# The norm folded into the router, the last two token tiles one by one, and VectorE's end ordered by hand, in a mixer and mixture-of-experts block

## The chip, the core and the metric

The kernel runs on one core of one Trainium2 chip. The metric is the device time of one launch in microseconds (us). The names in this text are those of the profile: PE is TensorE (PEld its weight load), DVE is VectorE, ACT is ScalarE, POOL is GpSimd, SP is SyncE. SP computes nothing here: it issues DMA transfers, one after the other, in the order of its program. POOL issues the indirect transfers and some plain ones.

## The reference

One post-norm layer over 1024 tokens of width 1024. A token mixer (differential attention beside a pooling mixer, merged by gates) ends in a product with `w_out`; then a layer norm, then a mixture of 32 experts in 4 groups of 8, then a second layer norm:

```
m   = merged @ w_out                                     # 1024x1024 @ 1024x1024
x1  = layer_norm(ALPHA * x + BETA * m)                   # ln1
g   = softmax(x1 @ w_router_group  + b_router_group)     # 4 groups, top 1
e   = softmax(x1 @ w_router_expert + b_router_expert)    # 8 experts of that group, top 2
f   = sum over the two chosen experts of
        weight * (silu(x1 @ w_gate[e]) * (x1 @ w_up[e])) @ w_down[e]      # width 512
out = layer_norm(ALPHA * x1 + BETA * f)                  # ln2
```

All values are float32. The kernel writes each wide product as three TensorE products of a high and a low part (`mm3`), and each weight is split into these parts on the chip by an ACT cast and a DVE subtraction (`split`).

## The kernel before

The mixer takes the first 800 us. What the change touches is the stretch behind it, here called the output stage, and what follows on it is the expert stage.

**Output stage.** The 1024 tokens lie in 8 tiles of 128. For a tile `j`, `mix` makes the product with `w_out` on PE in two halves of 512 columns (`n`), each over 8 blocks `k` with three matmuls into `pw`: 48 matmuls a tile. `residual` (DVE) adds `ALPHA * x` for one half and takes its statistics. After the second half `norm` calls `layer_norm` (DVE): mean and variance, a reciprocal root in steps, `x` minus mean times gain, a factor of -5/16 on the root, then two instructions of 512 columns for root and bias; POOL stores the tile to `X1`. Then come the routing steps of the tile:

- `turn`: 8 transposes on PE of the normalised tile (`px`), copied to `xT` by ACT; POOL scales the tile by `ALPHA` (L945) and stores it to `Y`, where the experts' results are added later.
- `route`: 8 matmuls (16 instructions in the trace) with the 36 router columns (`pr`, L820), then some 25 small DVE instructions that find the group, the two experts and the selection masks `M` and `Ms`; `weights` makes the two weights of the token.
- `places`: two small matmuls that count how many earlier tokens chose the same expert (L879, L880), and one-hot rows `ohr` (L884 to L890).
- `place`: matmuls that add the tile's tokens to the table `first` of each expert's tokens (L898), from which the indices `idx` for the experts' gathers are made at the end (L1013, L1014); for tiles 0 to 5 POOL stores the tile's rows of a table.

The order on PE and ACT is written out by hand: tiles are taken in the groups (0, 1), (2,), (3,), (4,), (5,), (6, 7), and the table `S5` says, for the last tile of a group, before which step `k` of its product a routing step stands. `S5_LATE` and `S5_END` hold what comes after the last product: both the transposes and the routing of tile 6, and all of tile 7's. DVE, POOL and SP are ordered by a scheduler.

**Expert stage.** Each expert takes 96 token rows: POOL gathers them from `X1` (L1089), PE transposes them (L1029), multiplies with gate and up (`gu`) and down (`dn`), and POOL adds the rows to `Y` by an indirect transfer (L1101). The weights of all experts come in 192 pieces of 1 MB (`we`, L1048), 6 an expert, all issued by SP in one queue. A piece waits in a buffer until ACT and DVE split it, in two halves, into one of 5 buffers `wh`. There are 16 buffers for pieces: 15 of a ring that the output stage also uses, and one more, `extra`, that takes piece 13 of every 16 (`M_AT`). Its memory lies where the output stage keeps small tensors and some of the split `w_out`:

```
w = slot([4, 512], F32, "we") if i % (NS + NM) not in M_AT else extra([4, 512], "we")
q = SP.dma_start(w, A["we"][expert[e], c].rearrange("p (k n) -> p k n", k=4))
```

The first 16 pieces are issued as early as their buffers come free, in the output stage. `layer_norm` of the second norm and the end follow after the last expert.

Of the kernel before, what the change touches and what calls it, by code (L numbers as in the profile page):

```python
# [57 lines left out]
S5_LATE = ((32, "turn", 6),)  # L58
S5 = {
    1: (),  # L60
    2: ((13, "turn", 0), (15, "route", 0)),
    3: ((1, "turn", 1), (3, "route", 1), (8, "places", 0), (11, "turn", 2), (13, "place", 0), (13, "route", 2), (14, "places", 1)),
    4: ((2, "place", 1), (4, "places", 2), (10, "turn", 3), (10, "place", 2), (12, "route", 3)),
    5: ((3, "places", 3), (10, "turn", 4), (10, "place", 3), (12, "route", 4)),
    7: ((3, "places", 4), (10, "turn", 5), (10, "place", 4), (12, "route", 5), (21, "places", 5), (26, "place", 5)) + S5_LATE,
}
S5_END = (("logits", 6), ("route", 6), ("turn", 7), ("weights", 6), ("logits", 7), ("route", 7), ("places", 6), ("weights", 7), ("place", 6), ("places", 7), ("place", 7))
# [12 lines left out]
P_GB, P_SUB, P_PS, P_N = 0, 16, 17, 21  # L80
# [26 lines left out]
def body(tc, ctx, A, out):  # L107
# [677 lines left out]
    def layer_norm(tiny, x, bs, y, g, b):  # L785

        mv = tiny([2], "mv")
        DVE.bn_aggr(mv, bs)
        v = tiny([4], "v")
        DVE.tensor_scalar(v[:, 0:1], mv[:, 1:2], EPS, None, op0=OP.add)  # L790
        steps = rsqrt_steps(v[:, 1:2], v[:, 0:1], v[:, 2:3])
        steps[0]()
        DVE.scalar_tensor_tensor(x, x, mv[:, 0:1], g, op0=OP.subtract, op1=OP.mult)
        steps[1]()
        steps[2]()
        DVE.tensor_scalar(v[:, 1:2], v[:, 1:2], -5.0 / 16, None, op0=OP.mult)
        for c in (slice(0, 512), slice(512, 1024)):
            DVE.scalar_tensor_tensor(y[:, c], x[:, c], v[:, 1:2], b[:, c], op0=OP.mult, op1=OP.add)

    wr = ph["S2"].tile([128, 8, 36], F32, name="wr")  # L800
    br = ph["S2"].tile([128, 36], F32, name="br")
    SP.dma_start(wr, A["wr"])
    SP.dma_start(br, bass.AP(tensor=A["br"].tensor, offset=0, ap=[[0, 128], [1, 36]]))

# [3 lines left out]
    def turned(x):  # L808
        xT1 = raw4([8, 128], "xT1")
        for g in range(2):  # L810
            px = p5.tile([128, 4, 128], F32, name=nm("px"), tag="X", bufs=2)
            for k in range(4):
                PE.transpose(px[:, k], x[:, (4 * g + k) * 128:(4 * g + k) * 128 + 128], ident)
            ACT.copy(xT1[:, 4 * g:4 * g + 4], px)
        return xT1

    def logits(xT1):
        pr = p5.tile([128, 512], F32, name=nm("pr"), tag="R", bufs=2)
        for k in range(8):
            PE.matmul(pr[:, :36], xT1[:, k], wr[:, k], start=k == 0, stop=k == 7)  # L820
        lg = tiny([36], "lg")
        DVE.tensor_add(lg, pr[:, :36], br)
        return lg, pr

    def route(j, lg, pr):

        s = tiny([16], "s")
        gm, ngm, sg = (s[:, i:i + 1] for i in range(3))
        DVE.tensor_reduce(gm, lg[:, 0:4], AX.X, OP.max)
        DVE.tensor_scalar(ngm, gm, -1.0, None, op0=OP.mult)  # L830
        eg, G = tiny([4], "eg"), tiny([4], "G")
        ACT.activation(eg, lg[:, 0:4], AF.Exp, bias=ngm, accum_out=sg)
# [3 lines left out]
        tg, fg = tiny([4], "tg"), tiny([1], "fg")  # L836
        DVE.tensor_reduce(mx[:, 0], le, AX.X, OP.max)
        DVE.scalar_tensor_tensor(tg, lg[:, 0:4], gm, down8[:, :4], op0=OP.is_equal, op1=OP.mult)
        for k in range(2):
            v = t[:, k]  # L840
            DVE.tensor_tensor(v, le, to(mx[:, k]), op=OP.is_equal)
            DVE.tensor_mul(v, v, down8[:, None, :].to_broadcast([128, 4, 8]))
            if k == 0:
                DVE.tensor_reduce(fg, tg, AX.X, OP.max)
                DVE.tensor_scalar(G, tg, fg, None, op0=OP.is_equal)
            DVE.tensor_reduce(f[:, k], v, AX.X, OP.max)
            DVE.tensor_tensor(oh[:, k], v, to(f[:, k]), op=OP.is_equal)
            if k == 0:
                big = tiny([4, 8], "big", bufs=1)
                DVE.scalar_tensor_tensor(big, oh[:, 0], NEG, le, op0=OP.mult, op1=OP.add)  # L850
                le = big
                DVE.tensor_reduce(mx[:, 1], le, AX.X, OP.max)
        M = tiny([2, NE], "M")
        for k in range(2):
            DVE.tensor_tensor(M[:, k].rearrange("p (g e) -> p g e", g=4), to(G), oh[:, k], op=OP.mult)
        Ms = tiny([NE], "Ms", BF)
        DVE.tensor_add(Ms, M[:, 0], M[:, 1])
        return M, Ms, pr, s, mx, G, eg

    def weights(j, s, mx, G, eg):  # L860

        gm, ngm, sg, me, gp, m1, m2, nm1, e2, w = (s[:, i:i + 1] for i in range(10))
        eq = tiny([2, 4], "eq", bufs=1)
        for k, m in enumerate((m1, m2)):
            DVE.scalar_tensor_tensor(eq[:, k], mx[:, k], 1.0, G, op0=OP.mult, op1=OP.mult, accum_out=m)
        DVE.tensor_reduce(me, eg, AX.X, OP.max)
        DVE.reciprocal(sg, sg)
        DVE.tensor_mul(gp, me, sg)
        DVE.tensor_scalar(nm1, m1, -1.0, None, op0=OP.mult)
        ACT.activation(e2, m2, AF.Exp, bias=nm1)  # L870
        DVE.tensor_scalar(w, e2, 1.0, None, op0=OP.add)
        DVE.reciprocal(w, w)
        DVE.tensor_mul(pay[:, j, 0, 2:3], w, gp)
        DVE.tensor_mul(pay[:, j, 1, 2:3], pay[:, j, 0, 2:3], e2)

    def places(j, M, Ms, pr):

        pp = pr[:, 256:288]
        PE.matmul(pp, tri, Ms, start=True, stop=False)  # L879
        PE.matmul(pp, one, cum, start=False, stop=True)  # L880
        oh = st([2, CAP + 2 * NE], "ohr")
        at = tiny([2], "at")
        for k in range(2):
            DVE.tensor_scalar(oh[:, k, CAP:CAP + NE], M[:, k], pay[:, j, 0, 3:4], None, op0=OP.mult)  # L884
            DVE.tensor_scalar(oh[:, k, CAP + NE:], M[:, k], pay[:, j, k, 2:3], None, op0=OP.mult)
        for k in range(2):
            t = tiny([NE], "pt", bufs=1)
            DVE.scalar_tensor_tensor(t, M[:, k], 1.0, pp, op0=OP.mult, op1=OP.mult, accum_out=at[:, k:k + 1])
        for k in range(2):
            DVE.tensor_scalar(oh[:, k, :CAP], slots, at[:, k:k + 1], None, op0=OP.is_equal)  # L890
        DVE.tensor_add(cum, cum, Ms)
        return M, pr, oh, at

    def place(j, M, pr, oh, at):
# [4 lines left out]
        DVE.tensor_add(first, first, pf.rearrange("p (c e) -> p c e", c=2))  # L899
# [5 lines left out]
        DVE.tensor_add(entry[:, j], sf, at)  # L905

# [26 lines left out]

    def norm(j):
        x = tl[j]["x"]
        layer_norm(tiny, x, tl[j]["s"], x, *lnp)
        POOL.dma_start(X1[j * 128:j * 128 + 128], x)

    def step(what, j):

        if what == "turn":
            x = tl[j]["x"]
            tl[j]["t"] = turned(x)
            y = slot2([D], F32, "yy") if j in Y_OUT else x
            POOL.tensor_scalar(y, x, ALPHA, None, op0=OP.mult)  # L945
            POOL.dma_start(Y[j * 128:j * 128 + 128], y)
        elif what == "route":
            if "l" not in tl[j]:
                tl[j]["l"] = logits(tl[j]["t"])
            tl[j]["m"] = route(j, *tl[j]["l"])  # L950
            if j < 6:
                weights(j, *tl[j]["m"][3:])
        elif what == "logits":
            tl[j]["l"] = logits(tl[j]["t"])
        elif what == "weights":
            weights(j, *tl[j]["m"][3:])
# [8 lines left out]
    with tc.manual_schedule(engines={mybir.EngineType.PE, mybir.EngineType.Activation}):  # L965
        for group in ((0, 1), (2,), (3,), (4,), (5,), (6, 7)):
# [4 lines left out]
            for n in range(2):  # L971
                for j in group:
# [355 lines left out]
def arrange(x, positions, w_in, gate_bias, lam_vecs, subln_gain, w_pool, pool_scale, w_branch_a, w_branch_b, w_out,  # L1328
# [56 lines left out]
    par[:, P_SUB] = a(subln_gain)[0]  # L1385
    par[:, P_PS:P_PS + 4] = a(pool_scale)[0].reshape(4, 128).T
# [29 lines left out]
```

## Time and profile before

| what | us |
|---|---|
| three runs: median (least, most) | 1566.15 (1562.53, 1566.98) |
| the profiled execution: its time, its span | 1564.77, 1563.0 |
| output stage, first to last start of a `pw` matmul | 808.8 to 923.49 |
| first gather of expert rows issued, first `gu` matmul | 942.58, 948.34 |
| last `dn` matmul of the expert stage | 1516.96 |
| PE busy in the span | 1488.5 (95%) |
| ACT waits for expert weights, 12 times in all | 8.4 |

Times of the trace count from the start of the span. The page's first lines give the busy time of each engine; a view by stretches gives the same for a window of time with the granted clock of TensorE and the share in which the core's 16 DMA engines were busy; the timeline gives single instructions, and in brackets how long the engine had been idle before one and what released it.

### The profile page before, as it was taken

The numbers are of one execution on the slowest core, as the hardware profiler recorded it, in microseconds if no ns is written. First come the engines' busy times: TensorE is split into PE (matmuls) and PEld (weight loads), VectorE is DVE, ScalarE is ACT, GpSimd is POOL, SyncE is SP. The second block draws the span as 40 slices with busy tenths as digits, with TensorE's granted clock in tenths as the row PEclk, the third lists the DMA queues.
The fourth block names the chain that finished last, engine by engine and source line by source line (L and its number), as shares of the span: only waits on it lengthen the run. The fifth ranks groups of instructions, "written<-read, shape, count | busy, mean of one in ns | idle before, by whom it ended". The sixth has DMA issues, their size and how long they took to land.

```text
span 1563.0 us, 22004 instructions
## 1 busy us (share of the span) xinstructions
PE 1488.5 (95%) x7627; PEld 1189.5 (76%) x7627; DVE 1195.1 (76%) x2284; ACT 945.3 (60%) x1571; POOL 277.3 (18%) x231
## 2 busy tenths in 40 slices
PE   8999999999999999999999988999999999999980
PEld 6988887798798898888888775777777777776750
DVE  5774214987988987775566788999989999898967
ACT  4323124665666766674341116888888888888864
POOL 0001000220210211100002544223222222211410
PEclk9999999999999999999999988999999999999995
DMA  6156224746856765618465477999999999999945
GB/s 237 56 175 201 81 75 101 222 152 170 231 184 176 215 188 144 150 67 312 150 256 208 171 261 256 383 370 375 375 374 356 362 364 357 366 352 377 396 147 215
DMA packets 116977, 375.46 MB, mean 240 GB/s; under 512 B 13767, under 2 KB 44871, under 8 KB 91504
## 3 DMA queue, kind: packets, MB, share of 16 engines
q1 hardware_dynamic: 76128, 303.25, 52.7%
q0 software_dynamic: 40160, 69.96, 17.3%
q8 instruction: 61, 1.00, 0.3%
q10 hardware_dynamic: 576, 0.83, 0.2%
q14 instruction: 52, 0.43, 0.1%
HBM read 312.44 MB, written 69.78 MB: 245 GB/s over the span
## 4 chain that ended last, share of the span: by engine, by line
PE 55%; issue 28%; POOL 9%; DVE 5%; ACT 1%; DMA 1%; POOLq 0%; DVEq 0%; SPq 0%; ACTq 0%
POOL Y L1101 7%; PE ps L570 4%; PE pg L162 4%; PE pg L163 4%; PE pg L164 4%; PE po L621 3%; PE pv L162 2%; PE pv L164 2%; PE pv L163 2%; PE tp L606 2%; POOL xg L1089 2%; PE pa L164 2%; PE pa L163 2%; PE pa L162 2%; PE pw L162 2%
## 5 line engine op out<-in xcount | busy, mean ns | idle before, releaser
L148 DVE TENSOR_TENSOR wh<-we,wh 128x1024 fp32r<-128x1024 f32 x384 | 459.7, 1219 | 54.1 <-ACT wh L147 50.5
L147 ACT CAST wh<-we 128x1024 fp32r<-128x1024 f32 x384 | 400.4, 1047 | 90.0 <-PE gu L164 51.5
L162 PE MATMUL gu<-wh,xT 128*96 128x512 f32 x512 | 204.3, 399 | 0.0
L164 PE MATMUL gu<-wh,xT 128*96 128x512 f32 x512 | 202.6, 396 | 0.6 <-DVE xT L148 0.6
L163 PE MATMUL gu<-wh,xT 128*96 128x512 f32 x512 | 201.8, 394 | 0.0
L1101 POOL DMA_INDIRECT Y<-y,idx x32 | 108.5, 3390 | 265.4 <-ACT y L1109 260.6
L148 DVE TENSOR_TENSOR w<-wraw,w 128x512 fp32r<-128x512 f32 x111 | 75.7, 685 | 92.1 <-ACT w L147 91.7
L147 ACT CAST w<-wraw 128x512 fp32r<-128x512 f32 x111 | 68.5, 621 | 115.1 <-PE pg L164 36.4
L573 ACT ACTIVATE P<-ps,stat 128x256 f32<-128x256 f32 (+7 forms) x128 | 94.8, 741 | 58.9 <-DVE stat L572 58.4
L164 PEld LDWEIGHTS gu<-wh,xT 128*96 128x96 f32 x512 | 83.0, 162 | 37.2 <-DVE xT L148 1.3
L163 PEld LDWEIGHTS gu<-wh,xT 128*96 128x96 f32 x512 | 83.3, 163 | 34.1 <-issue 0.5
L162 PEld LDWEIGHTS gu<-wh,xT 128*96 128x96 f32 x512 | 83.0, 162 | 33.2 <-ACT xT L147 0.2
L162 PE MATMUL dn<-wh,hT 128*96 128x512 f32 x256 | 102.4, 400 | 0.6 <-ACT hT L147 0.6
L570 PE MATMUL ps<-K,Q 128*128 128x512 f32 (+2 forms) x384 | 99.5, 364 | 1.2 <-DVE z L461 0.8
L164 PE MATMUL dn<-wh,hT 128*96 128x512 f32 x256 | 100.6, 393 | 0.0
L163 PE MATMUL dn<-wh,hT 128*96 128x512 f32 x256 | 100.6, 393 | 0.0
L162 PE MATMUL pg<-xT,w 128*128 128x512 f32 x256 | 100.4, 392 | 0.0
L163 PE MATMUL pg<-xT,w 128*128 128x512 f32 x256 | 100.0, 391 | 0.0
L164 PE MATMUL pg<-xT,w 128*128 128x512 f32 x256 | 99.9, 390 | 0.0
L572 DVE TENSOR_REDUCE stat<-ps 128x1 f32<-128x256 f32 (+7 forms) x128 | 95.3, 746 | 1.1
L570 PEld LDWEIGHTS ps<-K,Q 128*128 128x128 f32 x384 | 64.6, 189 | 10.8 <-DVE z L461 1.3
L162 PE MATMUL pv<-w,xT 128*128 128x256 f32 x256 | 72.8, 284 | 0.0
(277 smaller groups left out, 3395.3 us busy)
## 6 DMA issues: line engine op xcount, KB each, us to landing
we<-in_we_dram SPq DMA_DIRECT2D x192, 1024.0 KB, 23.5
wraw<-in_w_dram SPq DMA_DIRECT2D x61, 512.0 KB, 3.8
Q<-RQ POOLq DMA_DIRECT2D x64, 256.0 KB, 5.2
RQ<-rh SPq DMA_DIRECT2D x32, 256.0 KB, 3.3
K<-RK POOLq DMA_DIRECT2D x16, 512.0 KB, 5.5
V<-RV POOLq DMA_DIRECT2D x16, 512.0 KB, 5.7
OT<-ohl SPq DMA_DIRECT2D x48, 128.0 KB, 2.5
oT<-OT POOLq DMA_DIRECT2D x6, 1024.0 KB, 12.1
```

What stands on the lines that cost most here:

```text
L147: ACT.copy(hi, src)
L148: DVE.tensor_sub(lo, src, r(hi))
L162: PE.matmul(ps, a[0], b[0], start=start, stop=False)
L163: PE.matmul(ps, a[0], b[1], start=False, stop=False)
L164: PE.matmul(ps, a[1], b[0], start=False, stop=stop)
L570: PE.matmul(ps[:, c:c + n], q[:, o, m, qc], Kt[h, m][:, c:c + n], start=o == 0, stop=o == 1)
L572: DVE.tensor_reduce(st_[:, m:m + 1], ps[:, :W], AX.X, OP.max, negate=True)
L573: ACT.activation(Pt[h, i][m][:, :W], ps[:, :W], AF.Exp, bias=st_[:, m:m + 1], accum_out=st_[:, 2 + m:3 + m])
L606: PE.transpose(ps[:, k], p[:, (4 * g + k) * 128:(4 * g + k) * 128 + 128], ident)
L621: PE.matmul(o[:, 0, c], Vt[h][:, a, kt], aT[kt // 4][:, kt % 4, b, c], start=j == 0, stop=j == len(parts) - 1)
L1089: q = POOL.indirect_dma_start(out=x, out_offset=None, in_=X1, in_offset=IO(ap=idx[:, int(e < NXG), expert[e]:expert[e] + 1], axis=0), boun ...
L1101: q = POOL.indirect_dma_start(out=Y, out_offset=IO(ap=idx[:, 0, expert[e]:expert[e] + 1], axis=0), in_=y, in_offset=None, bounds_check=T - ...
```

## The change

It has three parts.

1. **The norm folded into the router.** `turn` transposes the tile before the norm (after the second residual). The router's weights are multiplied once by the gain (and by 5/16), on POOL, and `router`, 8 matmuls of 72 columns on PE, makes the column sums `wc` for the mean and the bias part that is added to `br`. `logits` becomes two DVE instructions (mean, then root and bias) in place of one. The factor of -5/16 is applied once to the gain, by ACT, and no more per tile. `centre` and `norm` follow the transposes.
2. **Tiles 6 and 7 one by one**, with a table `S5` that is new for all tiles. Tile 6's routing and half of tile 7's transposes stand between the products of tile 7.
3. **DVE's order written by hand** from tile 7's second residual on; `route` and `weights` are interleaved instruction by instruction, `entry` is made before `first`, and tile 7's scaling by `ALPHA` runs on ACT and no more on POOL.

```
-S5_LATE = ((32, "turn", 6),)
 S5 = {
     1: (),
-    2: ((13, "turn", 0), (15, "route", 0)),
...
-    7: ((3, "places", 4), (10, "turn", 5), (10, "place", 4), (12, "route", 5), (21, "places", 5), (26, "place", 5)) + S5_LATE,
+    2: ((3, "router", 0), (10, "turn", 0), (14, "route", 0)),
...
+    6: ((3, "places", 4), (4, "turn", 5), (8, "route", 5), (11, "place", 4)),
+    7: ((2, "places", 5), (4, "turn", 6), (7, "route", 6), (9, "place", 5), (11, "half", 7), (14, "places", 6)),
 }
-S5_END = (("logits", 6), ("route", 6), ("turn", 7), ("weights", 6), ("logits", 7), ("route", 7), ("places", 6), ("weights", 7), ("place", 6), ("places", 7), ("place", 7))
+S5_END = (("turn", 7), ("place", 6), ("centre", 7), ("root", 7), ("logits", 7), ("norm", 7), ("route", 7), ("places", 7), ("place", 7))
...
+    ACT.activation(lnp[0], lnp[0], AF.Copy, scale=-5.0 / 16)
...
+    wgb = slot([704], F32, "wgb")
+    w72, ones = wgb[:, :576].rearrange("p (k n) -> p k n", k=8), wgb[:, 576:]
+    POOL.memset(ones, 1.0)
+    for k in range(8):
+        g, b = (par[:, P_LN + 8 * i + k:P_LN + 8 * i + k + 1] for i in range(2))
+        POOL.tensor_scalar(w72[:, k, :36], wr[:, k], g, 5.0 / 16, op0=OP.mult, op1=OP.mult)
+        POOL.tensor_scalar(w72[:, k, 36:], wr[:, k], b, None, op0=OP.mult)
+    POOL.tensor_copy(wr, w72[:, :, :36])
+
+    def router():
+
+        pr = p5.tile([128, 512], F32, name=nm("pr"), tag="R", bufs=2)
+        for k in range(8):
+            PE.matmul(pr[:, :72], ones, w72[:, k], start=k == 0, stop=k == 7)
+        DVE.tensor_copy(wc, pr[:, :36])
+        DVE.tensor_add(br, br, pr[:, 36:72])
...
+    def turn(j, g):
+
+        x = tl[j]["x"]
...
+        px = p5.tile([128, 4, 128], F32, name=nm("px"), tag="X", bufs=2)
+        for k in range(4):
+            PE.transpose(px[:, k], x[:, (4 * g + k) * 128:(4 * g + k) * 128 + 128], ident)
+        ACT.copy(tl[j]["t"][:, 4 * g:4 * g + 4], px)
...
         lg = tiny([36], "lg")
-        DVE.tensor_add(lg, pr[:, :36], br)
+        mean, root = tl[j]["r"]
+        DVE.scalar_tensor_tensor(lg, wc, mean, pr[:, :36], op0=OP.mult, op1=OP.subtract)
+        DVE.scalar_tensor_tensor(lg, lg, root, br, op0=OP.mult, op1=OP.add)
         return lg, pr
...
+    def centre(j):
+        x = tl[j]["x"]
+        DVE.scalar_tensor_tensor(x, x, tl[j]["r"][0], lnp[0], op0=OP.subtract, op1=OP.mult)
+
     def norm(j):
-        x = tl[j]["x"]
-        layer_norm(tiny, x, tl[j]["s"], x, *lnp)
+        x, root = tl[j]["x"], tl[j]["r"][1]
+        for c in (slice(0, 512), slice(512, 1024)):
+            DVE.scalar_tensor_tensor(x[:, c], x[:, c], root, lnp[1][:, c], op0=OP.mult, op1=OP.add)
         POOL.dma_start(X1[j * 128:j * 128 + 128], x)
+        y = slot2([D], F32, "yy") if j in Y_OUT else x
+        if j == 7:
+            ACT.activation(y, x, AF.Copy, scale=ALPHA)
+        else:
+            POOL.tensor_scalar(y, x, ALPHA, None, op0=OP.mult)
+        POOL.dma_start(Y[j * 128:j * 128 + 128], y)
...
-        for group in ((0, 1), (2,), (3,), (4,), (5,), (6, 7)):
+        for group in ((0, 1), (2,), (3,), (4,), (5,), (6,), (7,)):
...
+                    if j == 7 and n:
+                        by_hand.close()
+                        by_hand.enter_context(tc.manual_schedule(engines={mybir.EngineType.PE, mybir.EngineType.Activation, mybir.EngineType.DVE}))
                     residual(j, n)
                     if n:
-                        norm(j)
+                        stats(j)
+                        if j < 7:
+                            root(j)
```

**What moves on SP.** The diff has no line on the loads of the expert weights, but SP's order is the scheduler's. These are SP's rows from the last load of `w_out` on, in the kernel before: pieces 0, 1, 2 and so on (`we_9574`, `we_9576`, ...), piece 12 (`we_9598`), piece 13 (`we_9631`, the one in the extra buffer) and piece 14.

```order
L198 DMA wraw_8114<-in_w_dram 128x1024 [waits DMAHW6_49,DMAHW5_49,DVE_49]
L1048 DMA we_9574<-in_we_dram 128x2048 [waits DMASW5_49,PE_49]
L1048 DMA we_9576<-in_we_dram 128x2048 [waits DMAHW7_49,PE_49]
L1048 DMA we_9578<-in_we_dram 128x2048 [waits DMAHW0_49,PE_49]
...
L1048 DMA we_9598<-in_we_dram 128x2048 [waits DMAHW2_49,DMASW2_49,PE_49]
L1048 DMA we_9631<-in_we_dram 128x2048 [waits DMAHW3_49,PE_49]
L1048 DMA we_9633<-in_we_dram 128x2048 [waits DMAHW4_49,DMASW3_49,PE_49]
```

In the changed kernel the same place reads as follows; `we_9666` is piece 13 (the extra buffer), `we_9609` is piece 0, `we_9633` piece 12 and `we_9668` piece 14.

```order
L199 DMA wraw_8114<-in_w_dram 128x1024 [waits DMAHW6_49,DMAHW5_49,DVE_49]
L1108 DMA we_9666<-in_we_dram 128x2048 [waits DVE_49,PE_49]
L1108 DMA we_9609<-in_we_dram 128x2048 [waits DMAHW7_49]
L1108 DMA we_9611<-in_we_dram 128x2048 [waits DMAHW0_49]
L1108 DMA we_9613<-in_we_dram 128x2048 [waits DMAHW1_49]
...
L1108 DMA we_9633<-in_we_dram 128x2048 [waits DMAHW3_49,DMASW2_49]
L1108 DMA we_9668<-in_we_dram 128x2048 [waits DMAHW4_49,DMASW3_49,PE_49]
```

Piece 13 has moved from behind piece 12 to the head of the queue, ahead of piece 0, and the waits for PE that pieces 0 to 12 had are no more on them. The extra buffer lies over `w_8128`, the part of the split `w_out` for `k=0, n=1`. The value that the row's wait on PE asks for is that of PE's last matmul that reads `w_8128`; in the changed kernel it is the last of the first three matmuls of tile 7's second half, shown here with the matmuls around it (`pw_9288` is tile 7's first half, `pw_9289` the second, `pr_9184` and `ohr_9299` are tile 5's placement).

```order
L165 MATMUL pw_9288<-wo_8142,mg_8063 128x512
L163 MATMUL pw_9289<-w_8128,mg_7593 128x512
L164 MATMUL pw_9289<-w_8128,mg_7593 128x512
L165 MATMUL pw_9289<-w_8128,mg_7593 128x512
L922 MATMUL pr_9184<-ohr_9299 96x64 [waits DVE_49] x2
L163 MATMUL pw_9289<-wo_8149,mg_7593 128x512
```

In both kernels 21 `pw` matmuls follow on these three; what stands among them is new.

**What moves on PE.** Before, PE's end of the output stage, from the last `pw` matmul on, holds the transposes of tile 6 (`px_9350`, `px_9356`) and tile 7 (`px_9426`, `px_9432`), then logits, places and placement of both tiles (`pr_9382` is tile 6, `pr_9453` tile 7), and then the transposes of the first gathered expert rows (`X`).

```order
L164 MATMUL pw_9100<-wo_8147,mg_8063 128x512
L813 MATMUL px_9350<-cst,xx_9092 128x128 [waits DVE_49,PE_49]
...
L820 MATMUL pr_9382<-wr,xT_9349 128x36 [waits Activation_49]
...
L813 MATMUL px_9426<-cst,xx_9097 128x128 [waits DVE_49,PE_49]
...
L820 MATMUL pr_9453<-wr,xT_9425 128x36 [waits Activation_49]
...
L879 MATMUL pr_9382<-Ms_9423,tri 128x32 [waits DVE_49]
...
L898 MATMUL pr_9382<-ohr_9498 96x64 [waits DVE_49] x2
...
L879 MATMUL pr_9453<-Ms_9494,tri 128x32 [waits DVE_49]
...
L898 MATMUL pr_9453<-ohr_9534 96x64 [waits DVE_49] x2
L1029 MATMUL X_9652<-cst,xg_9570 128x96 [waits DMASW2_49]
```

In the changed kernel only the second half of tile 7's transposes (`px_9485`), tile 6's placement (`pr_9352`) and tile 7's routing (`pr_9505`) stand behind the last `pw` matmul.

```order
L165 MATMUL pw_9289<-wo_8147,mg_8063 128x512
L821 MATMUL px_9485<-cst,xx_9286 128x128 [waits DVE_49]
...
L922 MATMUL pr_9352<-ohr_9450 96x64 x2
L827 MATMUL pr_9505<-wr,xT_9432 128x36 [waits Activation_49]
...
L900 MATMUL pr_9505<-Ms_9534,tri 128x32 [waits DVE_49]
...
L922 MATMUL pr_9505<-ohr_9564 96x64 [waits DVE_49] x2
L1089 MATMUL X_9687<-cst,xg_9605 128x96 [waits DMASW2_49]
```

Tile 6's transposes, logits and places, and the first half of tile 7's transposes, have moved up among the `pw` matmuls.

## Rows read from the trace of the kernel before

**Rows 1.** The page: span, and busy time, share and instructions of TensorE.

```profile
span 1563.0 us, 22004 instructions
PE 1488.5 (95%) x7627; PEld 1189.5 (76%) x7627; DVE 1195.1 (76%) x2284; ACT 945.3 (60%) x1571; POOL 277.3 (18%) x231
```

**Rows 2.** Busy time by stretches; last columns: granted clock, DMA share, GB/s.

```profile
core 0: us, PE busy (x) PEld busy (x) DVE busy (x) ACT busy (x) POOL busy (x), PEclk, DMA share, GB/s
916.00:960.00 44.00, 31.33 (x152) 24.74 (x151) 35.30 (x150) 16.70 (x30) 24.62 (x18) 0.73 0.75 247
...
1000.00:1100.00 100.00, 100.00 (x481) 71.36 (x480) 91.37 (x92) 84.43 (x101) 25.82 (x12) 1.00 1.02 376
...
1300.00:1400.00 100.00, 100.00 (x480) 71.38 (x479) 90.71 (x90) 84.14 (x101) 24.79 (x12) 1.00 1.01 359
```

**Rows 3.** Timeline of SP: start, us to the last issue's end, how many.

```profile
808.85 19.76 SPq L1048 DMA_DIRECT2D we<-in_we_dram  x6
...
860.04 7.16 SPq L1048 DMA_DIRECT2D we<-in_we_dram  x2
...
912.22 0.33 SPq L1048 DMA_DIRECT2D we<-in_we_dram  x1
918.65 0.33 SPq L1048 DMA_DIRECT2D we<-in_we_dram  x1
```

**Rows 4.** Timeline of TensorE around the end of the output stage: start, us.

```profile
918.23 0.40 PE L164 MATMUL pw<-w,mg 128*128 128x512 f32 x1
...
923.49 0.39 PE L164 MATMUL pw<-wo,mg 128*128 128x512 f32 x1
...
928.85 1.79 PE L813 MATMUL px<-cst,xx 128*128 128x128 f32 x8 [1.88 <-DVE xx L798]
930.46 3.63 PE L820 MATMUL pr<-wr,xT 128*128 128x36 f32 x16
...
946.87 1.54 PE L1029 MATMUL X<-cst,xg 96*128 96x96 f32 x8 [5.96 <-DMA xg<-X,idx]
948.34 0.74 PE L162 MATMUL gu<-wh,xT 128*96 128x512 f32 x1
```

**Rows 5.** DMA from 800 to 916 us: issues of expert weights, median us to landing.

```profile
we<-in_we_dram SPq DMA_DIRECT2D x13, 1024.0 KB, 6.0
```

**Rows 6.** DMA of three stretches: 916 to 960, 960 to 1000, 1000 to 1400.

```profile
DMA packets 2256, 10.87 MB, mean 247 GB/s; under 512 B 432, under 2 KB 432, under 8 KB 1431
...
GB/s 311 205 283 254 270 385 385 410 426 418 410 393 246 401 360 311 393 377 418 410 426 418 307 303 320 307 393 426 418 418 426 418 340 311 352 360 414 414 311 299
...
q1 hardware_dynamic: 18458, 134.41, 88.4%
```

**Rows 7.** Who waits for the expert weights: whole program, and from 1380 to 1450 us.

```profile
  DMA we<-in_we_dram: 8.4, 12
...
ACT wh L147 <- DMA we<-in_we_dram: 8.4, 12, 2.0
```

**Rows 8.** First and last start of `gu`, `dn` and gathers; landing of the gathers.

```profile
L162 PE MATMUL gu<-wh,xT x512: 389/392/739, 948.3 to 1504.1; 128*96 128x512 f32 x171
L164 PE MATMUL dn<-wh,hT x256: 388/393/469, 975.4 to 1517.0; 128*96 128x512 f32 x128
L1089 POOL DMA_INDIRECT xg<-X,idx x32: 960/981/2760, 942.6 to 1416.7; - x32
DMA to landing us min/median/max: 4.2/8.7/11.1
```

**Rows 9.** Timeline of TensorE, output stage, where it idles or runs at half clock.

```profile
849.07 2.33 PE L820 MATMUL pr<-wr,xT 128*128 128x36 f32 x16 [1.54 <-ACT xT L814]
...
864.90 0.63 PE L164 MATMUL pw<-wo,mg 128*128 128x512 f32 x1
865.33 0.63 PE L162 MATMUL pw<-wo,mg 128*128 128x512 f32 x1
...
885.14 0.18 PE L879 MATMUL pr<-Ms,tri 128*128 128x32 bf16 x1 [1.29 <-DVE Ms L857]
```

**Rows 10.** The chain that ended last: one logits step in the dense stretch.

```profile
907.60 1.71 PE pr L820 x16
```

More of the change, by code (lines that the diff above doesn't have):

```diff
@@ L783, in body @@
     p5 = ps5.__enter__()
[L785 to L798, printed above, removed]
+    ACT.activation(lnp[0], lnp[0], AF.Copy, scale=-5.0 / 16)
@@ L836, in route @@
         tg, fg = tiny([4], "tg"), tiny([1], "fg")
+        big, M, Ms = tiny([4, 8], "big", bufs=1), tiny([2, NE], "M"), tiny([NE], "Ms", BF)
+        tl[j]["m"] = M, Ms, pr, s, mx, G, eg
+        Mg = [M[:, k].rearrange("p (g e) -> p g e", g=4) for k in range(2)]
         DVE.tensor_reduce(mx[:, 0], le, AX.X, OP.max)
-        DVE.scalar_tensor_tensor(tg, lg[:, 0:4], gm, down8[:, :4], op0=OP.is_equal, op1=OP.mult)
[L839 to L856, printed above, removed]
+        DVE.tensor_reduce(gm, lg[:, 0:4], AX.X, OP.max)
+        DVE.tensor_tensor(t[:, 0], le, to(mx[:, 0]), op=OP.is_equal)
+        DVE.tensor_scalar(ngm, gm, -1.0, None, op0=OP.mult)
+        ACT.activation(eg, lg[:, 0:4], AF.Exp, bias=ngm, accum_out=sg)
+        DVE.tensor_mul(t[:, 0], t[:, 0], down8[:, None, :].to_broadcast([128, 4, 8]))
@@ L857, in route @@
+        yield
+        DVE.tensor_tensor(t[:, 1], big, to(mx[:, 1]), op=OP.is_equal)
+        yield
+        DVE.tensor_mul(t[:, 1], t[:, 1], down8[:, None, :].to_broadcast([128, 4, 8]))
+        yield
+        DVE.tensor_reduce(f[:, 1], t[:, 1], AX.X, OP.max)
+        yield
+        DVE.tensor_tensor(oh[:, 1], t[:, 1], to(f[:, 1]), op=OP.is_equal)
+        yield
+        DVE.tensor_tensor(Mg[1], to(G), oh[:, 1], op=OP.mult)
+        yield
         DVE.tensor_add(Ms, M[:, 0], M[:, 1])
-        return M, Ms, pr, s, mx, G, eg
@@ L884, in places @@
             DVE.tensor_scalar(oh[:, k, CAP:CAP + NE], M[:, k], pay[:, j, 0, 3:4], None, op0=OP.mult)
+        for _ in tl[j]["weights"]:
+            pass
+        for k in range(2):
             DVE.tensor_scalar(oh[:, k, CAP + NE:], M[:, k], pay[:, j, k, 2:3], None, op0=OP.mult)
@@ L905, in place @@
         DVE.tensor_add(entry[:, j], sf, at)
+        DVE.tensor_add(first, first, pf.rearrange("p (c e) -> p c e", c=2))
     def store_rows(j):
@@ L932, in residual, with stats, root @@
         DVE.bn_stats(tl[j]["s"][:, 6 * n:6 * n + 6], x[:, c])
+    def stats(j):
+        mv, v = tiny([2], "mv"), tiny([3], "v")
+        DVE.bn_aggr(mv, tl[j]["s"])
+        DVE.tensor_scalar(v[:, 0:1], mv[:, 1:2], EPS, None, op0=OP.add)
+        tl[j]["r"] = mv[:, 0:1], v[:, 1:2]
+        tl[j]["q"] = rsqrt_steps(v[:, 1:2], v[:, 0:1], v[:, 2:3])
+        tl[j]["q"][0]()
+    def root(j):
+        for s_ in tl[j]["q"][1:]:
+            s_()
+    def centre(j):
+        x = tl[j]["x"]
+        DVE.scalar_tensor_tensor(x, x, tl[j]["r"][0], lnp[0], op0=OP.subtract, op1=OP.mult)
@@ new lines, in norm @@
+        if j == 7:
[3 more added lines that the diff above has]
+        POOL.dma_start(Y[j * 128:j * 128 + 128], y)
+    def step(what, j):
+        if what == "router":
+            router()
+        elif what == "half":
+            turn(j, 0)
+        elif what == "turn":
+            for g in range(int(j == 7), 2):
+                turn(j, g)
+            if j < 7:
+                centre(j)
+                norm(j)
+        elif what in ("centre", "root", "norm"):
+            dict(centre=centre, root=root, norm=norm)[what](j)
@@ L947, in step @@
         elif what == "route":
             if "l" not in tl[j]:
[L949 to L952, printed above, removed]
+                tl[j]["l"] = logits(j)
+            steps_ = route(j, *tl[j]["l"])
+            next(steps_)
+            tl[j]["weights"] = weights(j, *tl[j]["m"][3:])
+            for _ in steps_:
+                next(tl[j]["weights"])
         elif what == "logits":
-            tl[j]["l"] = logits(tl[j]["t"])
-        elif what == "weights":
-            weights(j, *tl[j]["m"][3:])
+            tl[j]["l"] = logits(j)
@@ L962, in step @@
                 store_rows(j)
[L965 to L966 removed]
+    with ExitStack() as by_hand:
+        by_hand.enter_context(tc.manual_schedule(engines={mybir.EngineType.PE, mybir.EngineType.Activation}))
+        for group in ((0, 1), (2,), (3,), (4,), (5,), (6,), (7,)):
             for j in group:
```

60 lines of the change are left out of this document (31 added, 29 removed).

## The prediction

> **What bounds the kernel now.** I read the page first: PE is busy for 95% of the span [rows 1], so in most stretches time goes only if PE's work goes, or comes if PE waits. Then I asked stretch by stretch whether something else is close behind PE. In the expert stage it is the DMA: from 1000 to 1400 us its share is 1.01 to 1.02 while PE never idles [rows 2]. Two limits lie side by side there, and the reader should see which is the tighter one. PE takes 1517.0 - 948.3 = 568.7 us for 192 pieces of weights [rows 8], 2.96 us a piece, so 135 pieces in 400 us. The queue of the weights moved 134.41 MB in the 400 us from 1000 on [rows 6], which is 128 pieces of 1.0486 MB. The DMA falls behind by 7 pieces, some 20 us, and this runs down a reserve that was built up before. The reserve is gone near 1390: all 12 waits of ACT for weights lie between 1380 and 1450, 8.4 us in all [rows 7]. After 1417 the gathers are over [rows 8] and the DMA keeps up. So before, the reserve just reached to the end. It is worth about 20 us at 1000 us, and every microsecond taken from it must come back as a wait of PE.
>
> Where it comes from the timeline of SP shows: the first 13 pieces are issued between 808.85 and 912.22 us, in the output stage, as their buffers come free [rows 3], and land 6.0 us later in the median [rows 5].
>
> **The change, part by part.**
>
> *The head of the weights' queue.* In the changed order piece 13 stands ahead of piece 0. Its buffer lies over `w_8128`, so its issue waits for PE's third matmul of the last tile's second half. The trace of before shows this wait where it did no harm: that matmul starts at 918.23 and takes 0.40, and piece 13 is issued at 918.65 [rows 3, 4]. SP issues in order; now pieces 0 to 12 stand behind this wait. None of the 13 issues of 808.85 to 912.22 can happen there. They begin when tile 7 has come that far.
>
> The rows show one queue that issues in order; the Trainium skill ("DMA: Bandwidth & Descriptors", section "Anatomy of one DMA") says why: DMA engines do not wait on semaphores, any such wait happens on the issuing sequencer before dispatch. If by contrast each transfer could wait by itself, pieces 0 to 12 would go out as before and the sum would be that of the first rival below.
>
> When is that? The last `pw` matmul started at 923.49 [rows 4]. The output stage loses time before: PE idles 1.54 and 1.29 us, a logits step takes 2.33 us where it can take 1.71, and after two of these stops the clock falls, with matmuls 0.43 us apart (864.90 to 865.33) instead of 0.23 (918.23 to 918.46), some 14 of them [rows 9, 10]: 2.8 + 0.6 + 14 x 0.2 = 6.2 us. The new table leaves more matmuls between a step and the one that needs it. Moved in among the products come tile 6's transposes (8, about 0.8), its logits (1.71), half of tile 7's transposes (0.4) and `router` (8 matmuls of 72 columns, as a logits step: 1.7): 4.6 us. If the stalls all go, the last `pw` starts at 923.49 - 6.2 + 4.6 = 921.9; if they all stay, at 928.1. I take 922. The distance from the third matmul to the last was 5.26 us [rows 4]; 0.4 of transposes and less than 0.1 of counting come in, so the queue opens near 922 - 5.8 + 0.4 = 916.7 us (to 923).
>
> *What the lateness costs the DMA.* Twelve to 13 pieces of work move behind 916 us. One piece takes 2.5 us where only weights flow (1.0486 MB at 410 to 426 GB/s, [rows 6]): 30 to 32.5 us. What was free behind 916 takes part of it. From 916 to 960 the DMA moved 10.87 MB [rows 6], which at the 376 GB/s of a full stretch [rows 2] is 28.9 us of 44: 15.1 us free. By the share (0.75) it is 11 us. So the landings come 30 - 15.1 = 15 to 32.5 - 11 = 21.5 us later, plus 0.7 for an opening at 916.7. I take 16, near the lower end, since a share counts packets that wait too, and bytes do not.
>
> *What PE feels of it.* The reserve of 20 us at 1000 becomes 4. It is gone near 1080 instead of 1390, and from there until the gathers end the DMA sets the pace: 20 us a 400 us, over some 335 us, about 17. PE is not hurt by the first of it, since `wh` holds five split halves: before, ACT waited 8.4 us for weights and PE kept on. That cover is worth between 0 and 8.4 us; I take 3, as the longest single wait was 2.0 [rows 7]. The end comes 16 - 3 = 13 us later than in the trace.
>
> *What the change gains, and why it doesn't count.* In the tail, from 923.49 to the first `gu` at 948.34 [rows 4], before does tile 6's and tile 7's routing one through the other, PE idles 1.88 us for the normalised tile 7, and transposes and logits run at half clock, 1.79 and 3.63 us. Now tile 7's second half of transposes follows right behind its residual, and tile 6's logits and DVE steps are out of the way. By the row of logits this saves from 1.88 (the idle alone) to 10 us (923.49 to 934.09, where the logits end, less 0.7 of residual); about 5 is my estimate for the gather's issue. It meets a busier DMA: gathers took 4.2 us at least but 8.7 in the median [rows 8], so 4.5 of it is lost again if the weights then flow at full rate. With the 1.5 us of the earlier last product the first `gu` starts 2 us (to 7) earlier. As long as the weights set the pace this only makes PE wait longer for them.
>
> *The rest costs nothing that shows.* The 17 POOL instructions and the ACT scale of the gain come before the first norm, when both wait for data; a DVE instruction less (the -5/16) and one more (the logits) cancel; the scale of tile 7 moves from POOL to ACT, and both have nothing else of the path to do between the last norm and the first gather. Should the cover fail, a POOL delay of some 2 us would shift the first tile's load of `x`, which the matmuls of tiles 0 and 1 hide.
>
> **Sum.** On the profiled execution's own time, 1564.77 + 13 = 1577.8 us. Its time lies 1.4 us under the median of the runs shown; I keep 1578.
>
> **Rivals.**
>
> *The reserve suffices (faster).* If the loads catch up before they are needed, PE stays the bound and only the gains of the output stage count: 1564.8 - 2 to - 7, 1558 to 1563 us. For it: the first pieces are needed only from 948.34 on, one each 2.96 us [rows 4, 8], which an opening at 916.7 with 2.5 us a piece allows, and before ACT waited only 8.4 us. Against it: the reserve of 20 us was used up in the trace of before. It decides if the lateness at 1000 us is under some 3 us instead of 16, so if the free DMA time between 916 and 1000 were near 28 us; bytes give 15.
>
> *Half of it is hidden (no change).* A queue that is full from 916.7 on may deliver better than the average that I use: one piece each 2.4 us, and gathers beside it. With 2 us less of lateness from each of three terms (the pieces' pace, the free time, the cover) the end is 6 to 7 us later, less what the DMA wins after 1417, 0 to 3: 1568 to 1571.
>
> *More than forecast.* The output stage's stalls stay, the queue opens at 923 and landings are 22 us late: 1564.8 + 22 - 3 = 1584. Or PE, waiting a little for each piece, has its clock lowered for stretches as in [rows 9], where a matmul took 0.43 instead of 0.23 us: then PE is as slow as the weights or slower for such a stretch, and each 10 us of it cost up to 5. 1585 to 1600.
>
> On that side lies a rule of the Trainium skill ("DMA: Bandwidth & Descriptors", section "Where 436 GB/s comes from"): about 358 GB/s from HBM for one core, by which a piece would take 2.9 us, 13 pieces 38 us, and the end an estimated 1583. The trace does not agree: many slices stand at 410 to 426 GB/s.
>
> **How the numbers follow.** The forecast (13 us later, 8 to 20 with its bounds: 1572 to 1584) has a chance of 0.62; the worse case 0.18; half hidden 0.11; the reserve that suffices 0.09. What a measurement of this kernel can tell from no change is 0.3%, 4.7 us: faster is below 1561.45, slower above 1570.85. Of the 0.09 two thirds end below the first, 0.06; half hidden and the rest give 0.12 for the same; slower 0.82. The range that leaves out no more than 2 in 10: 1568 to 1588.
>
> **What would show it.** In the trace of the changed kernel: SP issues no expert weights before about 916 us, then 16 pieces close together; the DMA share is near 1 from there instead of 0.75; ACT's waits for weights begin between 1050 and 1200 instead of at 1390, and PE waits behind them, 10 us and more in sum; the first `gu` is no later than 948. It would be wrong if weights are issued from 809 us on, or if ACT does not wait for them before 1300.

## The result and the profile after

The changed kernel takes 1587.12 us (median of 5 runs, 1585.06 to 1588.78) against 1566.15. The medians lie 21.0 us apart; the ratio over all runs of both kernels is 1.0142, interval 1.0123 to 1.0161, so about 22 us slower. The forecast was 12 us slower. The mechanism came as forecast; its size was nearly double. The ratio on the median of before gives 1588.4, just over the range's upper end of 1588.

The page of the changed kernel, as [rows 1]: the span is 23.8 us longer, PE's busy time only 5.9.

```profile
span 1586.8 us, 22040 instructions
PE 1494.4 (94%) x7643; PEld 1185.7 (75%) x7643; DVE 1200.0 (76%) x2286; ACT 943.3 (59%) x1573; POOL 269.5 (17%) x248
```

The timeline of SP, to be read against [rows 3]: there is no load of expert weights before 922.42 us, then 17 issues in one row.

```profile
808.38 0.33 SPq L199 DMA_DIRECT2D wraw<-in_w_dram  x1
922.42 34.05 SPq L1108 DMA_DIRECT2D we<-in_we_dram  x17
```

What opened the queue stands in the timeline of PE, as [rows 4] for before: the third matmul that reads `w_8128` starts at 922.00 and takes 0.40; the first load follows at 922.42. Below it are the last product, the rest of tile 7's routing, and the first gathered rows.

```profile
922.00 0.40 PE L165 MATMUL pw<-w,mg 128*128 128x512 f32 x1
...
927.82 0.40 PE L165 MATMUL pw<-wo,mg 128*128 128x512 f32 x1
...
937.26 0.18 PE L900 MATMUL pr<-Ms,tri 128*128 128x32 bf16 x1 [4.98 <-DVE Ms L872]
...
939.08 0.90 PE L922 MATMUL pr<-ohr 128*96 128x64 f32 x4 [1.60 <-DVE ohr L914]
954.14 1.54 PE L1089 MATMUL X<-cst,xg 96*128 96x96 f32 x8 [14.16 <-DMA xg<-X,idx]
955.61 0.74 PE L163 MATMUL gu<-wh,xT 128*96 128x512 f32 x1
```

The busy time by stretches (the last columns as in [rows 2]), first a row of the kernel before, then rows of after. Until 916 the DMA's share is 0.28, where it was 0.58; from 916 to 960 it is 0.88, where it was 0.75. From 1000 on it stands at 1.00 to 1.02 as before, but now PE misses some per cent from 1200 us on: the count of its matmuls, 477, 451 and 442 in three stretches of 100 us, says this more plainly than the modelled busy time.

```profile
808.00:916.00 108.00, 104.49 (x535) 86.84 (x534) 76.77 (x387) 20.09 (x54) 37.66 (x35) 0.97 0.58 214
```

```profile
808.00:916.00 108.00, 105.02 (x546) 87.14 (x545) 82.33 (x400) 20.12 (x56) 48.05 (x53) 0.97 0.28 99
916.00:960.00 44.00, 22.11 (x121) 17.60 (x119) 28.96 (x136) 11.86 (x22) 18.57 (x16) 0.69 0.88 320
...
1100.00:1200.00 100.00, 100.00 (x477) 71.17 (x476) 88.35 (x88) 82.37 (x100) 21.30 (x12) 1.00 1.02 365
1200.00:1300.00 100.00, 96.80 (x451) 66.68 (x450) 85.82 (x88) 78.01 (x97) 18.76 (x10) 1.00 1.01 364
1300.00:1400.00 100.00, 95.69 (x442) 65.12 (x441) 84.77 (x85) 77.66 (x95) 20.11 (x11) 1.00 1.00 364
```

Who waits: ACT's waits for weights from 1000 to 1200 and from 1200 to 1540 us (in all, times, longest). Before it was 8.4 us, none of it ahead of 1380 [rows 7].

```profile
ACT wh L148 <- DMA we<-in_we_dram: 5.5, 7, 1.6
...
ACT wh L148 <- DMA we<-in_we_dram: 41.2, 44, 2.0
```

The queue of the weights from 808 to 1000 us (packets, MB, share), first a row of the kernel before, then one of after: 8.43 MB, 8.0 pieces, are missing at 1000 us.

```profile
q1 hardware_dynamic: 4664, 33.20, 47.6%
```

```profile
q1 hardware_dynamic: 3499, 24.77, 34.9%
```

From 1000 to 1400 the queue moves about the same in both kernels: 134.41 MB before [rows 6] and 135.21 MB after, 3.10 us a piece. So eight pieces are 25 us, and the end shows them: the last `dn` matmul, 1517.0 before [rows 8], starts 24.1 us later. Of these, 7.3 us stand already at the first `gu` (955.61 against 948.34), and from there to the last `dn` it takes 16.8 us longer.

```profile
q1 hardware_dynamic: 18566, 135.21, 88.6%
...
L165 PE MATMUL dn<-wh,hT x256: 388/393/475, 982.4 to 1541.1; 128*96 128x512 f32 x128
```

The theory that the runs test: the wait at the head of SP's queue is the whole loss, and it costs because the DMA is full for the whole expert stage and can't catch up. The rivals: the output stage itself is what costs (last product 4.3 us later, first `gu` 7.3 us later); the late start of the experts and the waits add up; or loads that start late end late, however much room there is.

### The profile page after: what moved, and what is told of

It is laid out like the page before. It is cut to its first block, busy times and chain, and to the rows that moved or that the text cites. A ratio compares the mean times of both kernels' runs of the same rounds, so it can differ in the third digit from the quotient of the medians.

```text
span 1586.8 us, 22040 instructions
## 1 busy us (share of the span) xinstructions
PE 1494.4 (94%) x7643; PEld 1185.7 (75%) x7643; DVE 1200.0 (76%) x2286; ACT 943.3 (59%) x1573; POOL 269.5 (17%) x248
## 4 chain that ended last, share of the span: by engine, by line
PE 52%; issue 31%; POOL 8%; DVE 5%; DMA 2%; ACT 1%; POOLq 0%; DVEq 0%; SPq 0%; ACTq 0%
POOL Y L1161 5%; PE ps L571 4%; PE pg L163 4%; PE pg L164 4%; PE pg L165 4%; PE po L622 3%; POOL xg L1149 3%; PE pv L163 2%; PE pv L165 2%; PE pv L164 2%; PE pa L165 2%; PE pa L164 2%; PE pa L163 2%; PE tp L607 2%; PE pB L164 2%
## 5 line engine op out<-in xcount | busy, mean ns | idle before, releaser
L148 ACT CAST wh<-we 128x1024 fp32r<-128x1024 f32 x384 | 395.3, 1047 | 116.8 <-DMA we<-in_we_dram 46.7
L1161 POOL DMA_INDIRECT Y<-y,idx x32 | 84.4, 2639 | 314.9 <-ACT y L1169 310.1
```

What stands on the lines that cost most here:

```text
L148: ACT.copy(hi, src)
L1161: q = POOL.indirect_dma_start(out=Y, out_offset=IO(ap=idx[:, 0, expert[e]:expert[e] + 1], axis=0), in_=y, in_offset=None, bounds_check=T - ...
```

## The experiments

Each ratio is to runs of the kernel before on the same chip.

**1. The queue in order.** One edit: each load of weights is issued behind the one before it.

```
+            with tc.issue_after(loads[-1].ins) if loads else ExitStack():
-            q = SP.dma_start(w, ...)
+                q = SP.dma_start(w, ...)
```

> The changed kernel with one thing taken back: piece 13 stands behind piece 12 in SP's queue again, as before. Theory (the head of the queue): the weights are issued from 809 us on, ACT's waits for them fall from 46.7 us to some 10, and nearly all of the 21 us go: 1562 to 1568 us. PE's output stage should end as in the changed kernel (last product near 928), the first gather no more waits behind weights for the store of its rows. Rival (the output stage itself, its last product 4.3 us later and the first gu 7.3 us later, is what costs): 1575 us or more.

Measured 1563.44 us, ratio 0.9999 (0.9987 to 1.0011): all of the loss is gone, though the last product comes no earlier (931.8, with the first load at 811.2). ACT's waits for weights are back at 8.9 us, and PE waits 6.27 us for the first gather instead of 14.16. These are lines of the views by tile (weights) and of PE's timeline:

```profile
L1110 SPq DMA_DIRECT2D we<-in_we_dram x192: 327/328/432, 811.2 to 1486.1; - x192
...
  DMA we<-in_we_dram: 8.9, 13
...
950.20 1.54 PE L1089 MATMUL X<-cst,xg 96*128 96x96 f32 x8 [6.27 <-DMA xg<-X,idx]
```

The rival that the output stage costs by itself falls.

**2. The kernel before with piece 13 first.** In `ahead`, piece 13 is taken ahead of pieces 0 to 12, and each load is issued behind the one before it, as in 1.

```
+            i = i if not 0 <= i <= 13 else 13 if i == 0 else i - 1
...
-    ahead(13)
+    ahead(14)
```

> The kernel before, with nothing but piece 13 put ahead of piece 0 in SP's queue. Theory: the queue opens at 918.7 instead of 922.4, so a little less late than the changed kernel: 1579 to 1587 us, ACT waits for weights from before 1250 on, some 40 us in all. Rival (the head of the queue does little): 1564 to 1570 us.

Measured 1601.4 us, ratio 1.0237 (1.022 to 1.0254): the same kind of loss, and larger than forecast. The timelines of SP and PE say why: in this kernel the load waits for later work than I took (I had 918.7). The queue opens only at 937.69, right behind the last placement matmuls of tile 7.

```profile
936.70 0.90 PE L898 MATMUL pr<-ohr 128*96 128x64 f32 x4 [1.49 <-DVE ohr L890]
...
937.69 31.39 SPq L1051 DMA_DIRECT2D we<-in_we_dram  x15
```

So it is a stronger dose than meant: the queue opens 15.3 us later than in the changed kernel, and the kernel takes 14.3 us longer.

**3. Half a dose: piece 13 behind piece 5.** As in 2, in the changed kernel, with 6 in place of 0, and each load behind the one before as in 1.

> The changed kernel with piece 13 behind piece 5, so that six pieces go out early and seven wait behind it: half a dose. Theory: lateness grows with the pieces that wait; about half of 28 us of later landings, of which the reserve and the split halves cover some: 1572 to 1579 us. A rival in which only the first pieces matter (the first expert starts late) says 1562 to 1568, as with the whole queue in order.

Measured 1578.08 us, ratio 1.0078 (1.0061 to 1.0095), as forecast; ACT waits 25.4 us for weights:

```profile
  DMA we<-in_we_dram: 25.4, 29
```

**4. VectorE's end left to the scheduler.** One step of the third part undone: DVE's end is no more ordered by hand. The rest of that part, such as the interleaving of `route` and `weights`, stays.

```
-                        by_hand.enter_context(tc.manual_schedule(engines={mybir.EngineType.PE, mybir.EngineType.Activation, mybir.EngineType.DVE}))
+                        by_hand.enter_context(tc.manual_schedule(engines={mybir.EngineType.PE, mybir.EngineType.Activation}))
```

> The changed kernel with one part undone: VectorE's order at the end is left to the scheduler. Nothing is said about the weights' queue, but in this build piece 13 stands behind piece 12 again. Theory (the head of the queue is the whole loss, and only this part of the change moved it): 1563 to 1568 us, weights issued from 809 us on; VectorE's end without the hand order costs 0 to 4 us. Rival (the fold or the tiles one by one cost by themselves): 1575 or more.

Measured 1563.33 us, ratio 1.0006 (0.9995 to 1.0018). The first load goes out at 810.6 again:

```profile
L1108 SPq DMA_DIRECT2D we<-in_we_dram x192: 327/328/551, 810.6 to 1483.2; - x192
```

So within the change it is the hand order of DVE with which the scheduler moves the load to the head of SP's queue, an engine that this step doesn't name; and that order gains nothing measurable over the scheduler's (compare run 1, which keeps it).

**5. No extra buffer.** `M_AT = ()`, 15 buffers.

> The changed kernel without the extra buffer: 15 buffers for pieces instead of 16, so no load waits for the memory of the split w_out at the head of the queue. Theory: nearly all of the loss goes; one buffer less takes some 3 us from the reserve, of which part shows: 1563 to 1570 us. Rival (the loss is not the wait at the head): 1575 or more.

Measured 1567.44 us, ratio 1.0034 (1.002 to 1.0047). The loss at the head is gone, and one buffer is worth some 4 to 5 us: ACT waits twice as long for weights as with 16.

```profile
  DMA we<-in_we_dram: 17.4, 21
```

**6. Piece 13 behind piece 9.** As 3, with 10.

> The changed kernel with piece 13 behind piece 9: three pieces that otherwise go out between 897 and 912 wait with it until about 922. Theory (lateness grows with the pieces that wait, three of 13, and part is covered): 1565 to 1571 us, between the queue in order (1563.4) and piece 13 behind piece 5 (1578.1). Rival (a threshold, any early hold costs alike): 1576 or more; or nothing, 1561 to 1565.

Measured 1570.11 us, ratio 1.0049 (1.0033 to 1.0064). With 3, 7 and 13 pieces held until about 922 us, the kernel is 0.5, 0.8 and 1.4% slower, 8, 12 and 22 us: graded, not a threshold. Here most of the loss isn't yet the reserve: ACT waits no more than with the queue in order, but POOL holds the first gather back for 8.5 us, and the first `gu` starts at 953.3, 4.1 us later than in run 4 (949.2). At the last `dn` the two are 6.0 us apart. Below are lines of the views by tile of the weights and of `gu` (run 6), then the `gu` line of run 4:

```profile
  DMA we<-in_we_dram: 8.7, 11
...
  POOL xg L1153: 8.5, 1
...
L163 PE MATMUL gu<-wh,xT x512: 389/393/739, 953.3 to 1510.3; 128*96 128x512 f32 x171
```

```profile
L163 PE MATMUL gu<-wh,xT x512: 387/393/741, 949.2 to 1504.3; 128*96 128x512 f32 x171
```

The profile puts the end of POOL's wait down to a load of weights. The gather itself needs the last store of `X1`, issued at 936.75, which took 9.2 us to land; that the wait is for this store, as in the changed kernel, is inferred.

**7. Another S5, queue in order.** For tiles 3 and 4:

```
-    3: ((2, "turn", 1), (5, "route", 1), (6, "places", 0), (10, "turn", 2), (13, "place", 0), (15, "route", 2)),
-    4: ((2, "places", 1), (5, "turn", 3), ...
+    3: ((2, "turn", 1), (8, "route", 1), (9, "places", 0), (10, "turn", 2), (14, "place", 0)),
+    4: ((1, "route", 2), (3, "places", 1), (5, "turn", 3), ...
```

> The queue in order and, beside it, another S5 for tiles 3 and 4: route of tile 1 at step 8 instead of 5, the places and placement of tile 0 later, route of tile 2 in tile 4. Theory (what ate the gain of the shorter end are the stalls in the output stage: 1.6 us until ACT's copy, then some 3 us at half clock, 1.0 us for first): the last product comes 3 to 5 us earlier than with the queue in order alone, and the time with it: 1558 to 1561 us. Rival (the stalls move to the next steps, or the weights bound the end anyway): 1562 to 1566.

Measured 1563.88 us, ratio 1.0008 (0.9997 to 1.0019): no gain. The wait for `xT` falls, and a new one stands in its place, for the DVE steps of tile 0's placement:

```profile
PE pr L827 <- DVE pt L926: 3.9, 2, 3.0
```

**8 and 9. A late start of PE**, once in the changed kernel, once with the queue in order.

```
+        idle = pt([512], "gu", 3, CAP)
+        for _ in range(30):
+            PE.matmul(idle, x[:, 0, 0], ring[0][:, 0, 0], start=True, stop=True)
```

> The changed kernel (piece 13 first) with 30 extra matmuls of 512 columns, whose result nobody reads, between the first transposes of gathered rows and the first gu: PE starts the experts some 7 us later. If the weights alone set the end of this kernel (a maximum of two paths), the late start is taken up by shorter waits for weights and the time stays near 1587 (to 1589). If the two losses add up (late start, then waits), 1592 to 1595 us.

> The same 30 matmuls with the queue in order. There PE sets the pace for most of the expert stage, so the late start should show nearly whole: 1563.4 + 4 to 7, 1567 to 1571 us; what it wins back is ACT's waits for weights, 8.9 us there, which should become fewer. If the weights set the end here too, 1563 to 1565.

Measured 1588.31 us (ratio 1.0153, 1.0138 to 1.0169) and 1573.21 us (1.0055, 1.0034 to 1.0076). In the changed kernel the late start costs 1 to 2 us; with the queue in order it costs about 9, above the forecast of 4 to 7. The price was wrong and not the path: the 30 matmuls, taken as 7 us, started at 957.6 (run 8) and 947.9 (run 9), and the `gu` behind them at 966.6 and 957.2, so they took 9.0 and 9.3 us. The longest of them took 0.74 us, the median 0.39. The first `gu` of the changed kernel goes from 955.6 to 966.6 (2 us of it because the whole output stage came later in this execution: its queue opened at 924.6), and ACT's waits for weights fall from 46.7 to 23.4 us: the late start only takes the place of waits.

```profile
L163 PE MATMUL gu<-wh,xT x512: 389/393/470, 966.6 to 1529.5; 128*96 128x512 f32 x171
L1271 PE MATMUL gu<-wh,xT x30: 387/392/739, 957.6 to 966.4; 128*96 128x512 f32 x30
...
  DMA we<-in_we_dram: 23.4, 27
```

So in the changed kernel the weights alone set the end. The late first `gu` and the waits are no two losses that add up.

**10. S5 once more, on kernel 4.** `places` of tile 0 stays at step 6, `route` of tile 1 at 8, `place` of tile 0 at 13, `route` of tile 2 at step 1 of tile 4.

> The changed kernel with VectorE's end left to the scheduler (queue in order by itself) and S5 spread in tiles 3 and 4: places of tile 0 stays at step 6, route of tile 1 goes from 5 to 8, route of tile 2 to step 1 of tile 4. If the stalls of the output stage (1.6 us for xT, 1.0 us for first, with the half clock behind) are what eats the shorter end, and the reserve of weights allows it: 1557 to 1561 us. If they move on again: 1562 to 1565.

Measured 1565.34 us, ratio 1.0009 (1.0 to 1.0018). The stalls move on again; what PE waits for from 800 to 960 us now (in all, times, longest) includes `entry`, and `Ms` twice:

```profile
PE pr L900 <- DVE Ms L872: 6.7, 2, 5.2
...
PE pr L827 <- DVE entry L928: 1.9, 1, 1.9
```

**11 and 12. Room on the DMA.** The changed kernel, and the kernel before, without 31 of the 32 additions of experts' rows to `Y`; most of the experts' results are left out of the output.

```
-        if n:
+        if n and e == 0:
             scatter(e, y)
```

> The changed kernel (piece 13 first) without 31 of the 32 indirect additions of experts' rows to Y, so that most of the experts' results are left out of the output and the DMA has some 2 us less to do for each expert. Theory (a late opening costs because the DMA is full for all the expert stage and can't catch up): with room the queue catches up, and what is left is the late first gu, 4 to 9 us over the kernel before without the same additions. Rival (loads that start late end late, whatever room there is): 18 us or more over it.

> The kernel before, without the same 31 additions (most of the experts' results are left out): the basis for the other one. PE should set the pace throughout, ACT wait for weights hardly at all (under 2 us instead of 8.4): 1556 to 1566 us.

Measured 1565.04 and 1557.35 us (ratios to the kernel before 1.0008, 0.9994 to 1.0023, and 0.9956, 0.9938 to 0.9975). The gap between the two orders shrinks from 22 to 7.7 us. The queue still opens late (923.7 us), but ACT's waits for weights in the changed kernel fall from 46.7 to 0.2 us (in the other there are none) and PE loses nothing from 1200 us on. The DMA's share is still 1.01 there, with fewer additions beside the loads:

```profile
  DMA we<-in_we_dram: 0.2, 1
...
1200.00:1300.00 100.00, 100.00 (x474) 71.07 (x473) 91.32 (x92) 85.06 (x103) 4.78 (x5) 1.00 1.01 386
```

What is left is about the late first `gu`, which starts 7.2 us apart in these two (956.7 and 949.5). The rival that late loads end late however much room there is falls.

```profile
L163 PE MATMUL gu<-wh,xT x512: 389/392/742, 956.7 to 1512.3; 128*96 128x512 f32 x171
```

```profile
L162 PE MATMUL gu<-wh,xT x512: 389/392/742, 949.5 to 1503.0; 128*96 128x512 f32 x171
```

No kernel that does all of the work beats the one before; 1, 4, 7 and 10 are level with it.

## What the prediction had right, and the steps that failed

**In short.** The mechanism held; the sum did not. It made the end 16 - 3 = 13 us later, and the trace shows 24.1. The step that failed is the lateness of the landings: 16 us were forecast, 8.0 missing pieces at 3.10 us are 25. The late opening of the queue gives about 4 of the 9 us between, the price of a piece about 5; the cover gives the other 2 of the 11.

**Right.** The place (piece 13 at the head of SP's queue, with the wait on `w_8128` ahead of pieces 0 to 12) is shown by the timeline of SP and by runs 1, 2 and 4. The reason why it hurts, a full DMA and a reserve that just reached to the end, is shown by 11 and 12, and by run 8 that the end is a maximum of two paths and no sum: a gain ahead of the experts counts for nothing while the weights are late. It was also right that the routing's end gets shorter: from the last product to the indices it takes 940.8 - 927.8 = 13.0 us, where before it took 941.8 - 923.5 = 18.3 us. The term for the free DMA time held too: at 922.4 us 14.1 MB of loads were missing against the kernel before (0.71 moved since 808 against 14.85), at 1000 us 8.43; the 5.7 MB between are 15 us at 376 GB/s, and 15.1 were forecast.

**Right in part by luck.** ACT's waits begin between 1050 and 1200 as said (all 7 of those ahead of 1200 lie behind 1150). But 25 us of lateness against a reserve of 20 would have emptied it by 1000. By these figures the experts' start, 7.3 us later and forecast the other way, gave back about as much (an estimate); the two errors worked against each other. What else kept the waits away until 1150 stays open.

**The opening of the queue** (the step that took 916.7, "I take 922" for the last product). It opened at 922.42, and the last product started at 927.82; the bound for stalls that all stay was 928.1. The new table had moved the stalls, not removed them. In the timeline of PE, as [rows 9]: a wait for `xT` with matmuls 0.43 us apart behind it, and a wait for `first`. The first of them leads to DVE as well: ACT's copy to `xT` stood behind an ACT instruction that waited 2.08 us for DVE.

```profile
852.28 2.32 PE L827 MATMUL pr<-wr,xT 128*128 128x36 f32 x16 [1.65 <-ACT xT L822]
...
854.98 0.63 PE L164 MATMUL pw<-wo,mg 128*128 128x512 f32 x1
855.41 0.63 PE L165 MATMUL pw<-wo,mg 128*128 128x512 f32 x1
...
878.15 1.95 PE L827 MATMUL pr<-wr,xT 128*128 128x36 f32 x16 [1.03 <-DVE first L929]
```

That more matmuls lie between two steps says nothing as long as DVE, which feeds them, is behind; I counted the distance on PE alone. Runs 7 and 10 show the same: each new table gave a new wait. These 5.7 us were a bound that I had, at the end that I did not take.

**The lateness of the landings** (16 us). I priced a displaced piece at 2.5 us, as where only weights flow. But pieces that are missing are missing in a stream that also carries a gather and an addition for each expert: there a piece takes 3.10 us. Eight pieces are missing at 1000 us, where 16 us at 2.5 meant 6.4; that is the late opening, which moved 13.5 pieces behind it and not 12. At 2.5 us the eight would be 20 us, at 3.10 they are 25. So 16 becomes 25; this is the term that was mis-sized.

**The cover** (3 us by `wh`). The end came 24.1 us later for 25 us of missing pieces, so by this difference it was worth about 1; no run measures it alone.

**The start of the experts** was forecast 2 us early, and no later than 948 as a sign, and came 7.3 us late. I had the gather under load (9.9 us here, 944.23 to 954.14, against 4.2), but not the store of tile 7 to `X1`, for which the first gather waits: issued at 934.70, and the gather is held until 944.23, while `idx` was ready at 940.8. POOL's timeline:

```profile
934.70 0.55 POOL L979 DMA_DIRECT2D X<-xx  x1 [10.16 <-DVE s L848]
...
944.23 1.05 POOL L1149 DMA_INDIRECT xg<-X,idx  x1 [7.92 <-DMA X<-xx]
```

In the changed kernel this cost little or nothing more (run 8); it is about what remains where the weights don't bind, in run 11, and much of it in run 6.

**Of the rivals**, the reserve that suffices and the half that is hidden did not come. "More than forecast" was the nearer one, and by its first branch: an opening at 923, with 1584 as its time, which had the price of a piece wrong as well. The branch on the clock did not come: the granted clock is 1.00 in every stretch from 960 us on.

The Trainium skill's sentence ("DMA: Bandwidth & Descriptors", section "Anatomy of one DMA") that waits are held by the issuing sequencer agrees with the traces: 17 loads issued in one row from 922.42 on, none ahead of it. The Trainium skill's 358 GB/s for one core (same page, section "Where 436 GB/s comes from") would have given a time nearer the measured one, an estimated 1583. The traces don't show that limit: between 930 and 948 us slices of the changed kernel's trace stand at 397 to 457 GB/s, and from 1000 to 1400 all its queues together moved 368 GB/s, 338 of it weights.

What stays open: why the scheduler puts the load first when DVE's end is ordered by hand was not followed, only that it does (run 4 against the changed kernel).

## What to carry to other kernels

Look at the whole order of each issuing engine after a change, also of those that the change doesn't name: one wait at the head of an in-order queue holds everything behind it, and a row moved by a scheduler can cost more than the edit gains. Where DMA and compute are both near full, ask for the reserve (how far ahead the loads are, and when it runs out), and price a missing transfer by the pace of the full stream with all its other traffic, not by its own duration. A step moved earlier on one engine removes a stall only if the engine that feeds it has time.

## What the runs showed of the hardware

While SP's loads kept the DMA full, a store of 512 KB issued by POOL held the gather behind it for 9.5 us (934.70 to 944.23), and that gather's rows took 9.9 us to reach PE (944.23 to 954.14). In the kernel before, the median for such stores was 3.8 us from issue to landing, and the first gather took 4.2. A load of 1 MB took 2.5 us where only loads flowed (410 to 426 GB/s, [rows 6]) and 3.10 us where a gather and an addition for each expert flowed beside them; most of the loss came back when the additions were left out (runs 11 and 12).
